# Down products in two halves of 256 columns, and sums of weight quarters on GpSimd

## The chip, the cores and the metric

The kernel runs on one core of one Trainium2 chip, in one launch. The metric is the device time of that launch in microseconds (us); lower is better. A core has TensorE (matrix products, PE in the profile; PEld is its weight loads), VectorE (DVE), ScalarE (ACT), GpSimd (POOL) and SyncE (SP), which issues the DMA transfers. Each engine works through its own queue in order, and semaphores tie the queues together.

## The reference, cut to what matters

One decoder block on 512 tokens of width 2048, all in float32: a projection, two attention mixers, an output projection, and then the feed-forward part (FFN), which the change touches:

```python
FFN_HIDDEN = 5632
...
    hn2 = rmsnorm(h, norm2_g[l])
    h = h + (jax.nn.silu(hn2 @ w_gate[l]) * (hn2 @ w_up[l])) @ w_down[l]
return rmsnorm(h, final_g)
```

## The kernel before, in words

**Three matmuls for one product.** A float32 operand is split into a high part in the format fp32r and a low part, the rest. A product of two operands is high x high, high x low and low x high, added up in PSUM. `mm3` issues these three (lines 165 to 167), and `mm` issues the same three for the gate and up products (lines 1010 to 1012). `ah` and `al` hold the high and low parts of the activations.

**Weights: jobs.** Weights come from memory as raw tiles by DMA on SyncE's queue (`load_to`, line 108, 512 KB each, four buffers `raw`; the down weights at line 736 into two buffers `rawd`). A `Job` makes one tile of 128 x 512 weights ready: `first` lets ScalarE write the high part `wh` (line 136), `second` lets VectorE write the low part `wl` = raw - high (line 139). A job may have a `prep`, issued before its high part, and a `post`, issued after its low part. `split_to` issues the jobs in a fixed order, three or four tiles ahead of TensorE; `wh` and `wl` have five buffers each. Nothing else plans the order: it is the order in which the program issues, engine by engine, and `later` puts evaluation steps some tiles behind the product they belong to. `wsplit` places the tile in its buffer at one of two offsets; jobs marked `even` take the other offset. In the FFN these are the first tile of blocks 1, 2, 5, 13, 21, 29 and 37.

**FFN by blocks.** The hidden width is cut into 44 blocks `f` of 128. For each block gate and up are one product of a 2 x 2 arrangement (two halves of the weights' rows, gate and up as columns; two halves of the tokens, 256 each), done with seven products P1 to P7 in place of eight. Each uses two weight tiles (halves `k`), so that a block has 14 tiles, each of 12 matmuls with 128 x 256 moving columns. The seven products need sums of the weight quarters A11, A21, A22, A12, which are formed in place in the raw tiles: `comb` (line 754). The order of products in a block is P1, P7, P4, P6, P5, P2, P3, and `quad_jobs` attaches the sums so: A11 += A21 ahead of P7, A21 += A22 behind P4's low part, A22 += A11 ahead of P6, A12 += A22 ahead of P3, each for both halves. In block 0 most sums are made by accumulating DMAs issued on GpSimd's queue instead (`fetch`, line 758, and line 112); one sum, ahead of P4, uses `comb` there too.

**Down products.** Four blocks' results lie in `ah[:, 12:16, :]`. In the block after them (blocks 4, 8, ..., 40) 16 down products for the 16 blocks of the model width are interleaved between the seven products; three or four follow each of P7 to P2. `down` takes one weight tile and fills one PSUM bank of 512 columns with 12 matmuls; one tile later VectorE adds the bank to `hs` (line 1077). The last four blocks' down products are made in `last`, which works in halves of 256 columns already and has 24 sums of squares on GpSimd (line 1125).

**After a product.** `after` combines the products' PSUM banks on VectorE (lines 1033, 1036, 1055: one operand in PSUM) and multiplies by the norm factor (line 1060, both operands in SBUF); `finish` makes silu (line 1017), gate x up (line 1020), and the high and low part of the result (lines 1021 and 1025).

Of the kernel before, what the change touches and what calls it, by code (L numbers as in the profile page):

```python
# [14 lines left out]
OP = mybir.AluOpType  # L15
# [8 lines left out]
PH = 4  # L24
# [47 lines left out]
def block_kernel(ctx: ExitStack, tc: tile.TileContext, xt, wst, wdn, smalls, wg, w2c, bias, ident_in, out):  # L72
# [3 lines left out]
    pe, act, dve, pool_e, sp = nc.tensor, nc.scalar, nc.vector, nc.gpsimd, nc.sync  # L76
# [13 lines left out]
    ah = slot["h"][:, MH:MH + KB * S].rearrange("p (a b) -> p a b", b=S)  # L90
    al = slot["l"][:, ML:ML + KB * S].rearrange("p (a b) -> p a b", b=S)
# [10 lines left out]
    def load_to(n):  # L102
        while state["dma"] < min(n, len(units)):
            u = state["dma"]
            t = wp.tile([128, 1024], F32, tag="raw", name="raw", bufs=LA)
            for k in range(2 if u < TWO else 1):
                c = slice(512 * k, 512 * k + 512) if u < TWO else slice(0, 1024)
                sp.dma_start(t[:, c], wst[u][:, c])
            raws[u] = t
            state["dma"] += 1  # L110
            if units[u] == ("quad", 0, 1):
                pool_e.dma_start(t, wst[u + 1], accum_op=OP.add)
# [51 lines left out]
    def mm3(o, wh, wl, mh, ml, start, stop):  # L164
        pe.matmul(o, wh, mh, start=start, stop=False)  # L165
        pe.matmul(o, wh, ml, start=False, stop=False)  # L166
        pe.matmul(o, wl, mh, start=False, stop=stop)  # L167
# [4 lines left out]
    def next_half():  # L172
        i = pos["half"]
        pos["half"] += 1
        split_to(i + (AHEAD[i] if i < len(AHEAD) else 3 if i < len(jobs) - KB - 1 else 4))
        if i < n_plain:
            load_to(i // 2 + LA)
        while lag and lag[0][0] <= i:
            lag.popleft()[1]()
        j = jobs[i]  # L180
        return j.h, j.l

    def later(n, f):
        i = len(lag)
        while i and lag[i - 1][0] > pos["half"] + n:
            i -= 1
        lag.insert(i, (pos["half"] + n, f))
# [109 lines left out]
    for k in range(KB):  # L297
        x = xc.pop(k)
# [353 lines left out]
    def proj_block(upto=None):  # L652
        return ps.tile([128, 512], F32, tag="proj", name="pp", bufs=2)
# [40 lines left out]
    for j in range(NH):  # L694
# [5 lines left out]
        p = proj_block()  # L700
# [3 lines left out]
        o = {}  # L704
# [4 lines left out]
        p = proj_block()  # L709
# [3 lines left out]
        p = proj_block()  # L713
# [5 lines left out]
        p = proj_block()  # L719
# [20 lines left out]
    def load_fin(n):  # L740
        while len(fin) < min(n, KB // 2):
            k = 2 * len(fin)
            fin.append(wp.tile([128, 1024], F32, tag="raw", name="fin", bufs=LA))
            sp.dma_start(fin[-1].rearrange("p (n c) -> p n c", n=2), wdn[NPH - 1, k:k + 2].rearrange("n p c -> p n c"))

    def quad_jobs(f, order):

        u = base_u + 4 * f

        def q(i, k):  # L750
            return raws[u + i][:, 512 * k:512 * k + 512]

        def comb(o, x):
            return lambda: dve.tensor_tensor(o(), o(), x(), op=OP.add)  # L754

        def fetch(o, i, k):

            return lambda: pool_e.dma_start(o(), wst[u + i][:, 512 * k:512 * k + 512], accum_op=OP.add)

        def nxt(i):  # L760
            return lambda: load_to(u + 4 + i + 1)

        r = {}
        for k in range(2):
            A11, A21, A22, A12 = (lambda i=i, k=k: q(i, k) for i in range(4))

            if f == 0:
                r["P1", k] = Job(A11, load=None if k else nxt(-1), post=fetch(A11, 1, k))
                r["P5", k] = Job(A21, post=fetch(A21, 0, k))
                r["P7", k] = Job(A11)  # L770
                r["P2", k] = Job(A12)
                r["P4", k] = Job(A22, prep=comb(A12, A21))
                r["P6", k] = Job(A21)
                r["P3", k] = Job(A12)
            else:
                r["P1", k] = Job(A11)
                r["P7", k] = Job(A11, prep=comb(A11, A21))
                r["P4", k] = Job(A22, post=comb(A21, A22))
                r["P5", k] = Job(A21)
                r["P6", k] = Job(A22, prep=comb(A22, A11))  # L780
                r["P2", k] = Job(A12)
                r["P3", k] = Job(A12, prep=comb(A12, A22))
        if f + 1 < FB:
            if f == 0:
                r["P6", 1].post = nxt(2)
                r["P3", 1].post = nxt(3)
            else:
                r["P6", 1].post = nxt(0)
                r["P5", 1].post = nxt(1)
                r["P3", 1].post = nxt(3)  # L790
        else:
            r["P6", 1].post = lambda: load_fin(1)
            r["P5", 1].post = lambda: load_fin(2)
            r["P3", 1].post = lambda: load_fin(LA)
        r["P1", 0].even = f in (1, 2) or f % 8 == 5
        return [r[p, k] for p in order for k in range(2)]
# [14 lines left out]
    for f in range(FB):  # L811
        qj = quad_jobs(f, ORDER if f else ORDER0)
        p = f // PH - 1
# [16 lines left out]
    def out_unit(half, tag="proj"):  # L830
        p = ps.tile([128, 512], F32, tag=tag, name="pab", bufs=2)
        c = 8 - 8 * half
        run_unit([(p, ah[:, c + k, :], al[:, c + k, :], k == 0, k == 7) for k in range(8)])
        return p
# [54 lines left out]
    for nb in range(KB):  # L889
        while "hs" not in rest and (nb == 4 and not idle() or nb == 2 and (queue or cur["s"])):  # L890
            step()
        p = out_unit(1, ("proj", "sc", "t")[nb // 2 % 3])
# [13 lines left out]
    LO, HI = slice(0, 256), slice(256, 512)  # L906
# [72 lines left out]
    for i in range(KB):  # L979
        nb = PASS2[i]  # L980
        p = out_unit(0)
# [27 lines left out]
    def mm(o, wh, wl, mh, ml, start, stop):  # L1009
        pe.matmul(o, wh, mh, start=start, stop=False, skip_group_check=True)  # L1010
        pe.matmul(o, wh, ml, start=False, stop=False, skip_group_check=True)  # L1011
        pe.matmul(o, wl, mh, start=False, stop=stop, skip_group_check=True)  # L1012
# [50 lines left out]
    def down(ph, nb):  # L1063
        n = nb % (3 if ph else 2)
        if n not in dbanks:
            dbanks[n] = banks["P3"] if not n else (ps.tile([128, 512], F32, tag="t", name="pd", bufs=2) if n == 1 else
                                                ps.tile([128, 512], F32, tag="misc", name="pd"))
        p = dbanks[n]
        h, l = next_half()
        for i in range(PH):  # L1070
            mm3(p, h[:, 128 * i:128 * i + 128], l[:, 128 * i:128 * i + 128], ah[:, 12 + i, :], al[:, 12 + i, :],
                i == 0, i == PH - 1)

        def add():
            if not ph:
                dve.tensor_tensor(hs[:, nb, :], hs[:, nb, :], st["inv"], op=OP.mult)
            dve.tensor_tensor(hs[:, nb, :], hs[:, nb, :], p, op=OP.add)  # L1077

        later(1, add)

    for kind, a, b in sched:
        if kind == "d":
            down(a, b)
            continue
        f, name = a, b
        product(f, name)
        if f == 0:
            if name == "P7":
                r = st["rs2"] = Rsqrt(tokens(sacc), D, rab.v[:, :4])
                r.invert()  # L1090
                dve.tensor_tensor(r.z, r.z, rab.y[:, :4], op=OP.mult)
                later(1, lambda r=r: st.update(inv=Spread(r.z), r2=Spread(r.y)))
            if name == "P6":
                st["inv"] = st["inv"](False)
                act.activation(st["rs2"].rs[:, 7, :1], ones[:, :1], AF.Silu)
                st["r2"] = st["r2"](tag="t", bufs=2)
                st["u"] = ft()
            if name in ("P1", "P6", "P3"):
                later(0 if name == "P1" else 1, lambda name=name: after(0, name))
        elif name in ("P1", "P6", "P5", "P2", "P3"):  # L1100
            later({(FB - 1, "P2"): 0, (FB - 1, "P3"): 3}.get((f, name), 1), lambda f=f, name=name: after(f, name))
# [144 lines left out]
```

## Time and profile before

| | |
|---|---|
| median of 3 runs | 2187.98 us (2187.74 to 2190.23) |
| the profiled execution, its time | 2189.1 us |
| its span, first to last instruction | 2187.3 us |
| mean granted TensorE clock | 0.997 |
| VectorE's sums, line 754 | 346, 237.4 us busy |
| down products in PSUM, matmuls of 512 columns in the loop | 160 x 12 |
| DMA | 33.0% of 16 engines' span, 105 GB/s |

A row of the groups gives line, engine and operation, what is written and read with its shape, the count, then busy time in us and the mean duration in ns, then the engine's idle time before it and what ended most of it. A row of the timeline gives start and duration in us, engine, line and operation. Consecutive instructions of one engine overlap at their ends: a duration is longer than the distance from start to start. For TensorE the distance between starts is called the pace here. A row of a tile's view gives shortest, median and longest duration in ns.

### The profile page before, as it was taken

Reading aid. Unit: us, or ns where it says so; the run is one execution under the profiler, and the core shown is the slowest. Engines: PE = TensorE matmul, PEld = TensorE weight load, DVE = VectorE, ACT = ScalarE, POOL = GpSimd, SP = SyncE. Lnnn points to the kernel's source line nnn. Section 1 sums busy time; section 2 is a strip of 40 time slices with the busy share of each in tenths; the row PEclk is TensorE's granted clock in tenths of the full one; section 3 lists DMA queues with packets and bytes.
Section 4 is the critical chain, followed back from the end, with each engine's and each line's share of the span. In section 5 each row is a group of like instructions: output and inputs, shape, how many; then the busy total and the mean of one; then the engine's idle time right before and its main releaser. Section 6 shows DMA issues by size and latency. Waiting matters only on the chain.

```text
span 2187.3 us, 35901 instructions
## 1 busy us (share of the span) xinstructions
PE 2167.3 (99%) x13856; PEld 1947.6 (89%) x13856; DVE 1568.5 (72%) x3045; ACT 971.0 (44%) x1862; POOL 43.7 (2%) x51
## 2 busy tenths in 40 slices
PE   9999999999999999999999999999999999999997
PEld 7788888888887889989899999989898999999897
DVE  6755656356667578979687777868696877778685
ACT  6544444344444255535343443435353434434356
POOL 0000000000000000000000000000000000000003
PEclk9999999999999999999999999999999999999998
DMA  6442222322224334333333333333333333333233
GB/s 223 145 137 80 80 80 68 101 88 80 65 92 154 98 97 106 121 111 97 107 107 111 92 116 107 102 93 122 109 97 107 107 111 97 112 106 102 90 120 106
DMA packets 82972, 232.04 MB, mean 106 GB/s; under 512 B 8816, under 2 KB 13296, under 8 KB 82800
## 3 DMA queue, kind: packets, MB, share of 16 engines
q1 hardware_dynamic: 82080, 228.17, 33.0%
q0 software_dynamic: 720, 1.57, 0.5%
q8 instruction: 109, 1.79, 0.3%
q14 instruction: 63, 0.52, 0.1%
HBM read 225.51 MB, written 4.19 MB: 105 GB/s over the span
## 4 chain that ended last, share of the span: by engine, by line
PE 96%; DVE 2%; ACT 1%; DMA 0%; issue 0%; SPq 0%; DVEq 0%; ACTq 0%
PE P L1010 13%; PE P L1011 13%; PE P L1012 13%; PE pp L165 6%; PE pp L167 6%; PE pp L166 6%; PE pd L167 4%; PE pd L166 4%; PE pd L165 4%; PE P L167 3%; PE P L166 3%; PE pab L166 3%; PE pab L167 3%; PE pab L165 3%; PE P L165 3%; PE pt L515 1%
## 5 line engine op out<-in xcount | busy, mean ns | idle before, releaser
L136 ACT ACTIVATE wh<-raw 128x512 fp32r<-128x512 f32 x888 | 549.4, 630 | 513.6 <-PE P L1011 172.0
L139 DVE TENSOR_TENSOR wl<-raw,wh 128x512 fp32r<-128x512 f32 x888 | 597.1, 686 | 62.7 <-ACT wh L136 62.2
L1012 PE MATMUL P<-ah,wl 128*128 128x256 f32 x1056 | 291.7, 276 | 0.3 <-DVE wl L139 0.3
L1010 PE MATMUL P<-ah,wh 128*128 128x256 f32 x1056 | 291.7, 276 | 0.0
L1011 PE MATMUL P<-al,wh 128*128 128x256 f32 x1056 | 291.6, 276 | 0.0
L165 PE MATMUL pp<-ah,wh 128*128 128x512 f32 x640 | 260.4, 407 | 0.0
L167 PE MATMUL pp<-ah,wl 128*128 128x512 f32 x640 | 250.9, 392 | 0.0
L166 PE MATMUL pp<-al,wh 128*128 128x512 f32 x640 | 250.2, 391 | 0.0
L754 DVE TENSOR_TENSOR raw<-raw 128x512 f32<-128x512 f32 x346 | 237.4, 686 | 3.4
L136 ACT ACTIVATE wh<-rawd 128x512 fp32r<-128x512 f32 x160 | 101.3, 633 | 280.5 <-PE pd L166 162.6
L1011 PEld LDWEIGHTS P<-al,wh 128*128 128x128 f32 x1056 | 198.2, 188 | 0.9
L1010 PEld LDWEIGHTS P<-ah,wh 128*128 128x128 f32 x1056 | 198.2, 188 | 0.8
L1012 PEld LDWEIGHTS P<-ah,wl 128*128 128x128 f32 x1056 | 198.2, 188 | 0.5 <-DVE wl L139 0.5
L1077 DVE TENSOR_TENSOR hs<-hs,pd 128x512 f32<-128x512 f32 x98 | 67.4, 688 | 131.4 <-PE pd L167 131.3
L167 PE MATMUL pd<-ah,wl 128*128 128x512 f32 x392 | 154.4, 394 | 0.0
L166 PE MATMUL pd<-al,wh 128*128 128x512 f32 x392 | 153.7, 392 | 0.0
L165 PE MATMUL pd<-ah,wh 128*128 128x512 f32 x392 | 152.1, 388 | 0.0
L167 PEld LDWEIGHTS pp<-ah,wl 128*128 128x128 f32 x640 | 120.2, 188 | 27.9
L165 PEld LDWEIGHTS pp<-ah,wh 128*128 128x128 f32 x640 | 120.5, 188 | 19.6
L166 PEld LDWEIGHTS pp<-al,wh 128*128 128x128 f32 x640 | 120.6, 188 | 19.5
L139 DVE TENSOR_TENSOR wl<-rawd,wh 128x512 fp32r<-128x512 f32 x160 | 109.8, 686 | 23.8 <-ACT wh L136 23.5
L504 ACT ACTIVATE e<-e,st 128x512 f32<-128x512 f32 (+1 forms) x96 | 54.2, 565 | 135.2 <-DVE st L502 135.2
(281 smaller groups left out, 4922.4 us busy)
## 6 DMA issues: line engine op xcount, KB each, us to landing
raw<-in_wst_dram SPq DMA_DIRECT2D x311, 512.0 KB, 3.5
rawd<-in_wdn_dram SPq DMA_DIRECT2D x160, 256.0 KB, 2.6
bias<-in_bias_dram SPq DMA_DIRECT2D x16, 320.0 KB, 3.0
xc<-in_xt_dram SPq DMA_DIRECT2D x16, 256.0 KB, 2.9
hs<-in_xt_dram SPq DMA_DIRECT2D x16, 256.0 KB, 5.2
fin<-in_wdn_dram SPq DMA_DIRECT2D x8, 512.0 KB, 3.7
out_dram<-hs SPq DMA_DIRECT2D x10, 256.0 KB, 2.2
out_dram<-hs SPq DMA_DIRECT2D x3, 512.0 KB, 3.4
```

Of the source, the lines that this page charges most:

```text
L136: act.activation(self.h, self.src(), AF.Copy)
L139: dve.tensor_tensor(self.l, self.src(), self.h.bitcast(F32), op=OP.subtract)
L165: pe.matmul(o, wh, mh, start=start, stop=False)
L166: pe.matmul(o, wh, ml, start=False, stop=False)
L167: pe.matmul(o, wl, mh, start=False, stop=stop)
L504: act.activation(et, et, AF.Exp, bias=m, scale=-1.0, accum_out=den)
L515: pe.transpose(p[:, 128 * (o + b):128 * (o + b) + 128], self.e[t][:, 128 * b:128 * b + 128], ident)
L754: return lambda: dve.tensor_tensor(o(), o(), x(), op=OP.add)
L1010: pe.matmul(o, wh, mh, start=start, stop=False, skip_group_check=True)
L1011: pe.matmul(o, wh, ml, start=False, stop=False, skip_group_check=True)
L1012: pe.matmul(o, wl, mh, start=False, stop=stop, skip_group_check=True)
L1077: dve.tensor_tensor(hs[:, nb, :], hs[:, nb, :], p, op=OP.add)
```

## The change

Two edits. In `quad_jobs`, `comb` issues its sums on GpSimd instead of VectorE; jobs and order are the same. In `down`, the bank is filled in two passes over the four weight slices, first the columns 0 to 255 (`LO`), then 256 to 511 (`HI`), by `mm` instead of `mm3` (the same three matmuls, in the form that the gate and up products use): 24 matmuls of 256 columns in place of 12 of 512.

```diff
--- before
+++ after
@@ -751,7 +751,7 @@
             return raws[u + i][:, 512 * k:512 * k + 512]
 
         def comb(o, x):
-            return lambda: dve.tensor_tensor(o(), o(), x(), op=OP.add)
+            return lambda: pool_e.tensor_tensor(o(), o(), x(), op=OP.add)
 
@@ -1067,9 +1067,10 @@
         p = dbanks[n]
         h, l = next_half()
-        for i in range(PH):
-            mm3(p, h[:, 128 * i:128 * i + 128], l[:, 128 * i:128 * i + 128], ah[:, 12 + i, :], al[:, 12 + i, :],
-                i == 0, i == PH - 1)
+        for c in (LO, HI):
+            for i in range(PH):
+                mm(p[:, c], h[:, 128 * i:128 * i + 128], l[:, 128 * i:128 * i + 128], ah[:, 12 + i, c],
+                   al[:, 12 + i, c], i == 0, i == PH - 1)
```

## The prediction

> **What bounds the kernel now.** I read the page first: the span, and how much of it TensorE is busy.
>
> ```profile
> span 2187.3 us, 35901 instructions
> ## 1 busy us (share of the span) xinstructions
> PE 2167.3 (99%) x13856; PEld 1947.6 (89%) x13856; DVE 1568.5 (72%) x3045; ACT 971.0 (44%) x1862; POOL 43.7 (2%) x51
> ```
>
> TensorE sets the time; VectorE has 28% to spare and GpSimd does nothing. The profiled execution took 2189.1 us, 1.8 us more than its span, and stands 1.1 us above the median of 2187.98; I add my sum to the median. A change of 0.2% (4.4 us) is about what can be told from none.
>
> Both edits lie in the feed-forward part, so next I read TensorE's rows in the timeline there, at the first matmul of two blocks that have no down products, two blocks apart.
>
> ```profile
> 1108.76 0.28 PE L1010 MATMUL P<-B11h,wh 128*128 128x256 f32 x1
> ...
> 1146.84 0.28 PE L1010 MATMUL P<-B11h,wh 128*128 128x256 f32 x1
> ```
>
> Two blocks take 38.08 us, one 19.04: 168 matmuls at 113.3 ns, without a pause. So VectorE's relief can save nothing in such a block; it can only be lost again.
>
> **Part 1: the halves.** 160 down products (10 phases of 16; the last phase has its own code) are 1920 matmuls of 512 columns now, and 3840 of 256 after. The pace of the wide form, 36 matmuls from the first row to the second; then that of the narrow form with the very operand of the edit, `ah[:, 12+i, c]`, in the last phase, 144 matmuls:
>
> ```profile
> 931.03 0.39 PE L165 MATMUL P<-ah,wh 128*128 128x512 f32 x1
> ...
> 939.27 0.28 PE L1010 MATMUL P<-T4h,wh 128*128 128x256 f32 x1
> ```
> ```profile
> 2130.80 0.28 PE L165 MATMUL pl<-ah 128*128 128x256 f32 x1
> ...
> 2147.11 0.28 PE L165 MATMUL pl<-ah,T1h 128*128 128x256 f32 x1
> ```
>
> 8.24/36 = 228.9 ns against 16.31/144 = 113.3 ns. Two halves take 226.6 ns, 2.3 ns less than one whole: 1920 x 2.3 = 4.4 us saved, all of it on the path. Weights are loaded twice as often, as the products do already at this pace; a weight tile is let go at its 23rd of 24 matmuls instead of its 11th of 12, 0.1 us later, which costs nothing while tiles are ready ahead. The add at L1077 waits for the whole bank as before. The Trainium skill's page "TensorE: Matmul & The Clock Gate", section "Back-to-back issue gap", gives an isolated gap of N/2.4 + 2.5 ns, by which two halves cost 2.5 ns more than one whole; the estimate from that would be +4.8 us instead of -4.4. The rows say otherwise, as long as TensorE keeps this pace.
>
> It doesn't always. Around 876 us, in the first block after block 0:
>
> ```profile
> 872.86 0.28 PE L1010 MATMUL P<-T4h,wh 128*128 128x256 f32 x1
> ...
> 875.58 0.28 PE L1010 MATMUL P<-ah,wh 128*128 128x256 f32 x1
> ...
> 876.26 0.39 PE L1012 MATMUL P<-ah,wl 128*128 128x256 f32 x1 [0.30 <-DVE wl L139]
> ...
> 878.96 0.28 PE L1010 MATMUL P<-T1h,wh 128*128 128x256 f32 x1
> ...
> 881.79 0.28 PE L1010 MATMUL P<-B21h,wh 128*128 128x256 f32 x1
> ...
> 890.23 0.28 PE L1010 MATMUL P<-ah,wh 128*128 128x256 f32 x1
> ...
> 892.95 0.28 PE L1010 MATMUL P<-T4h,wh 128*128 128x256 f32 x1
> ```
>
> Up to 875.58 24 matmuls take 2.72 us (113.3 ns). Then P6 waits for a low part on VectorE. From 878.96 on 24 take 2.83 us (117.9 ns), and from 890.23, after the first tile of block 2, which is placed `even`, 2.72 again. So a pause on TensorE puts the narrow form into a slower pace, 4.6 ns a matmul, until the next `even` tile, which comes with blocks 1, 2, 5, 13, 21, 29 and 37 only. No other pause happens in this part before.
>
> **Part 2: the sums on GpSimd.** What leaves VectorE, and what a block without downs has there (the window is one block; the 15th L139 is a neighbour's):
>
> ```profile
> L754 DVE TENSOR_TENSOR raw<-raw 128x512 f32<-128x512 f32 x346 | 237.4, 686 | 3.4
> ```
> ```profile
> L139 DVE TENSOR_TENSOR wl<-raw,wh 128x512 fp32r<-128x512 f32 x15 | 10.1, 687 | 1.0 <-ACT wh L136 1.0
> L754 DVE TENSOR_TENSOR raw<-raw 128x512 f32<-128x512 f32 x8 | 5.5, 687 | 0.1
> L1033 DVE TENSOR_TENSOR ft<-ft,P 128x256 f32<-128x256 f32 x3 | 1.3, 419 | 0.1
> L1036 DVE TENSOR_TENSOR ft<-ft,P 128x256 f32<-128x256 f32 x2 | 0.8, 421 | 0.1
> L1020 DVE TENSOR_TENSOR ft<-ft 128x512 f32<-128x512 f32 x1 | 0.7, 684 | 0.0
> L1025 DVE SCALAR_TENSOR_TENSOR al<-ft,ah 128x512 fp32r<-128x512 f32 x1 | 0.7, 684 | 0.0
> L1060 DVE TENSOR_TENSOR ft<-ft,r 128x256 f32<-128x256 f32 x1 | 0.4, 424 | 0.0
> L1055 DVE TENSOR_TENSOR ft<-P,r 128x256 f32<-128x256 f32 x1 | 0.4, 414 | 0.0
> ```
>
> 346 = 43 x 8 + 2: two sums of block 0 (before its P4) move too. On GpSimd the same form, seen before only in attention, and what VectorE does beside it:
>
> ```profile
> L649 POOL TENSOR_TENSOR acc<-acc,osq x14: 1276/1316/1930, 250.5 to 678.7; 128x512 f32<-128x512 f32 x14
> ```
> ```profile
> 263.65 1.28 POOL L649 TENSOR_TENSOR acc<-acc,osq 128x512 f32<-128x512 f32 x1 [11.74 <-ACT osq L648]
> ...
> 264.12 1.36 DVE L438 TENSOR_TENSOR qbl<-tmp,qbh 128x512 fp32r<-128x512 f32 x1 [2.79 <-ACT qbh L437]
> ```
>
> One sum takes 1.28 us when undisturbed, against 0.69. And VectorE's instruction, which reads two SBUF tensors like L139 (0.69 us), took 1.36: it ended at 265.48, 0.55 us after GpSimd's end at 264.93. It stood still while GpSimd ran. This is the rule against this change: the Trainium skill's "SBUF — State Buffer", section "SBUF: two separate sides", says that VectorE and GpSimd share a port pair as an exclusive lock, held for a whole instruction by a VectorE operation with two SBUF inputs or by GpSimd's. The trace agrees: 1.36 us instead of 0.69; had the two engines shared the port without loss, the sum would be Part 1 alone.
>
> So the two engines take turns. Budget of a block without downs: GpSimd 8 x 1.28 = 10.2 us; VectorE's two-SBUF instructions (14 L139, L1020, L1025 at 0.55 behind a turn of GpSimd, L1060 0.4) 9.2 us. Sum 19.4, against 19.04 for TensorE. The six PSUM instructions (L1033, L1036, L1055; under 0.42 each, 2.5 in all) can lie beside GpSimd where the order allows.  Blocks with downs (one in four, 44 us longer on TensorE) have ample room. So each three blocks in a row start with full lead and use it up.
>
> How much lead is there? Block at 1127.81:
>
> ```profile
> 1127.94 0.64 ACT L136 ACTIVATE wh<-raw 128x512 fp32r<-128x512 f32 x1 [0.72 <-PE P L1011]
> ...
> 1128.89 0.69 DVE L139 TENSOR_TENSOR wl<-raw,wh 128x512 fp32r<-128x512 f32 x1
> ...
> 1133.24 0.28 PE L1010 MATMUL P<-T4h,wh 128*128 128x256 f32 x1
> ...
> 1134.44 1.89 DVE L139 TENSOR_TENSOR wl<-raw,wh 128x512 fp32r<-128x512 f32 x3
> ...
> 1135.96 0.28 PE L1010 MATMUL P<-ah,wh 128*128 128x256 f32 x1
> ```
>
> P4's first high part starts when TensorE frees its buffer, 5.3 us before its matmuls. The tight place is P6, the one that paused at 876: between P4's first low part and P6's second stand four of the eight sums, alternating with low parts. P6's second tile starts at 1135.96 + 1.36 = 1137.32 and needs its low part at the third matmul, 1137.55; today that (the first of the three at 1134.44) is done at 1135.1, 2.4 us early. In turns, from the start of P1: the first P4 sum ends at 0.8, P7's second low part at 1.4, L1033 and L1060 at 2.1, P4's low parts at 2.7 and 3.3, P6's first sum at 4.4, L1020 at 5.0, P4's second sum at 6.1, P6's first low part at 6.7, P6's second sum at 7.8, its high part (0.64) at 8.5, its low part at 9.1. Needed at 9.7: 0.7 us left in the first block after the downs. Carried on the same way the turns need, as an estimate, 19.85 us a block (19.4 and the gaps in which one engine waits for the other's result), 0.8 more than TensorE: -0.1 in the second block, -0.9 in the third. TensorE pauses about once per three blocks, at P6, and the pause brings the 117.9 ns. At that pace a block takes 19.8 us, and the turns about keep up: the loss is mostly the pace.
>
> GpSimd's queue: its DMA issues of block 0 (five, the last at 846) stand ahead of the sums, the 24 adds of the last phase (L1125) behind them; nothing else waits there. A later sum also frees weights later, and SyncE waits for that:
>
> ```profile
> SPq L108 <- DVE raw L754: 497.9, 83, 14.6
> ```
> ```profile
> raw<-in_wst_dram SPq DMA_DIRECT2D x311, 512.0 KB, 3.5
> ```
> ```profile
> 1120.64 0.68 DVE L754 TENSOR_TENSOR raw<-raw 128x512 f32<-128x512 f32 x1
> ```
>
> The last sum of a block ends at 1121.3 and P4 of the next reads the new weights at 1127.94: 6.6 us for a load of 3.5. A sum up to 3 us later is hidden; I find 0.3 to 2.4. Cost nothing; if the cover is gone it is the same pause at P4.
>
> Sum. Slow pace: first from P6 of block 3 to block 4, then in each stretch between `even` tiles from P6 of the second block (6 and so on) on: 6.6 of 8 blocks x 168 x 4.6 ns = 5.1 us, and two phases of downs, 384 x 117.9 ns = 45.3 instead of 192 x 228.9 ns = 43.9 each, 2.7: 7.8 us, four times, 31; the short stretches at both ends 2.5 + 5.6; the last phase up to its norm 192 x 4.6 ns = 0.9. Together 40. The six pauses that begin it at 0.46 us (876.26 - 875.69, less 0.11) 3, later ones 2. +45: 2188 + 45 = 2233. Bounds of this case: pauses in only half of the stretches, the others with Part 1's gain, 2188 + 22 - 2 = 2208; turns of 20.4 us a block, 33 x 0.6 us more than the slow pace covers, 2253.
>
> **Rivals.** *No pause* (0.16): the order lets GpSimd run ahead, the 0.7 us hold; for it: 28% spare on VectorE, the P6 slack of 2.4; against: 19.4 us of turns in 19.04. Then only Part 1 is left, 2183.6, on either side of the 0.2%; this one ends on the other side. It decides at P6's second low part of the third block: earlier than TensorE by any margin. *Halves that cost* (0.03, also without pauses): a fixed cost per matmul comes back in the down order; at 117.9 ns in the downs alone, 3840 x 117.9 - 1920 x 228.9 = +13 us, 2201. The page's gap gives 2193 there. *Pauses, but the pace holds* (0.13): up to 0.1 + 0.9 us per three blocks, 11 times, to twice that, less 4.4: 2195 to 2206. For it: only one pause in this part is on record. *Heavy turns* (0.15): the PSUM instructions don't overlap and a block takes 19.4 + 2.5 = 21.9 us: 33 blocks x 2.9 less 11 x 1 us of lead, 85, and the slow pace in ten blocks with downs, 10 x (0.8 + 1.4) = 22: 2188 + 107 = 2295; half overlapped some 2255. *Turned pace*, the forecast: 0.53.
>
> **The numbers.** 2233, the likeliest. No pause is left out below (0.16), and the far end of heavy turns above (0.04): 2190 to 2275. No pause splits evenly at 0.2%: faster 0.08, same 0.08, slower 0.84.
>
> **What would show it.** Right: POOL busy near 500 us with L754 above 1.28 us; L139's mean above 687 ns; TensorE waits for `wl` at P6 in the second or third block of a cycle; 117.9 ns behind them until the next `even` tile; down halves at 113.3 ns only where no pause came before. Wrong: blocks of 19.04 us throughout and 2183; or L139 still at 687 ns beside GpSimd, so that the lock is not held against this form; or pauses after which 113.3 ns goes on.

## The result, and the profile after

The changed kernel takes 2289.88 us (median of 4 runs, 2288.57 to 2290.33) against 2188.06 before: ratio 1.0462, 95% interval 1.0449 to 1.0474, slower by 102 us. That is above the range; the direction was right. The profiled execution took 2290.33 us, its span 2288.6, so 101.3 us lie between the two profiled spans. The sums below are for the feed-forward part, where 99.9 of them arise.

The head of the page, then the groups of VectorE and GpSimd over the whole span:

```profile
span 2288.6 us, 39977 instructions
## 1 busy us (share of the span) xinstructions
PE 2227.3 (97%) x15776; PEld 2078.9 (91%) x15776; DVE 1532.1 (67%) x2699; ACT 955.4 (42%) x1862; POOL 554.6 (24%) x397
```
```profile
L139 DVE TENSOR_TENSOR wl<-raw,wh 128x512 fp32r<-128x512 f32 x888 | 722.9, 835 | 155.2 <-ACT wh L136 146.6
L754 POOL TENSOR_TENSOR raw<-raw 128x512 f32<-128x512 f32 x346 | 511.0, 1495 | 864.8 <-DVE wl L139 552.9
```

The 346 sums went over to GpSimd as said (511.0 us busy there), and VectorE lost instructions but hardly any busy time (1532.1 after 1568.5): its L139 went from 687 ns to 835. From here on only the feed-forward part is compared, from block 1's first matmul to the first `pl` matmul of the last phase. VectorE's groups there, after:

```profile
L139 DVE TENSOR_TENSOR wl<-raw,wh 128x512 fp32r<-128x512 f32 x600 | 530.6, 905 | 138.7 <-ACT wh L136 130.6
...
L1020 DVE TENSOR_TENSOR ft<-ft 128x512 f32<-128x512 f32 (+1 forms) x44 | 66.0, 1499 | 0.0
L1033 DVE TENSOR_TENSOR ft<-ft,P 128x256 f32<-128x256 f32 x131 | 54.4, 416 | 4.4 <-PE P L1012 1.8
```

Two SBUF operands: 905 and 1499 ns, from 687 and 679. One operand in PSUM (L1033): 416, from 419, untouched.

What TensorE waited for, in all, how often, and the longest:

```profile
PE P L1010 <- ACT ah L1021: 22.2, 10, 2.7
PE P L1012 <- DVE wl L139: 14.6, 17, 1.5
...
PE P L1011 <- DVE al L1025: 4.2, 10, 0.4
```

The second row is P6, where the forecast had its pauses. The first and third are new: at the first down product of each of the ten phases TensorE waits for `ah` and `al`, the moving operand.

To account for all of it I took each distance between two neighbouring matmul starts, less 113.33 ns for a narrow and 228.9 ns for a wide one. A small excess (up to 30 ns) is pace; distances of 200 to 225 ns are counted as narrow matmuls at half the clock; all else is a pause. (Some 15 of the 144 in the column of the halved clock, 1.6 us, lie where the granted clock is full, and are short waits.)

| feed-forward part, us | length | pace | halved clock | pauses |
|---|---|---|---|---|
| before | 1259.8 | 0.9 | 0.1 | 0.6 |
| after | 1359.7 | 39.3 | 14.5 (144 matmuls) | 52.1 |

With the 4.3 us that the halves save at full pace, 39.3 + 14.5 + 52.1 - 4.3 - 1.6 = 100.0; measured 99.9. Of the pauses 17.4 are P6's (17 times) and 30.8 the first downs' (23.8 for `ah`, 7.0 for `al`).

**P6.** The timeline of block 2, TensorE's rows, then VectorE's, then GpSimd's:

```profile
893.12 0.28 PE L1010 MATMUL P<-T4h,wh 128*128 128x256 f32 x1
...
895.84 0.28 PE L1010 MATMUL P<-ah,wh 128*128 128x256 f32 x1
...
897.29 0.39 PE L1012 MATMUL P<-ah,wl 128*128 128x256 f32 x1 [1.06 <-DVE wl L139]
...
899.99 0.28 PE L1010 MATMUL P<-T1h,wh 128*128 128x256 f32 x1
...
902.81 0.28 PE L1010 MATMUL P<-B21h,wh 128*128 128x256 f32 x1
```
```profile
892.46 1.38 DVE L139 TENSOR_TENSOR wl<-raw,wh 128x512 fp32r<-128x512 f32 x1 [0.62 <-ACT wh L136]
893.76 1.78 DVE L1020 TENSOR_TENSOR ft<-ft 128x512 f32<-128x512 f32 x1
895.46 1.77 DVE L139 TENSOR_TENSOR wl<-raw,wh 128x512 fp32r<-128x512 f32 x1
```
```profile
891.99 4.70 POOL L754 TENSOR_TENSOR raw<-raw 128x512 f32<-128x512 f32 x3 [2.09 <-DVE wl L139]
```

Three sums on GpSimd stretch three VectorE instructions of 0.69 us to 1.38, 1.78 and 1.77. GpSimd ends at 896.69 and the last L139 at 897.23, 0.54 us later: turns. TensorE reads that low part at 897.29 instead of 896.07, and 24 matmuls take 2.82 us from 899.99 where they took 2.72 from 893.12: behind the pause the slow pace has begun.

The same kind of pause can also end the slow pace. In block 15:

```profile
1304.06 0.28 PE L1010 MATMUL P<-T4h,wh 128*128 128x256 f32 x1
...
1306.89 0.28 PE L1010 MATMUL P<-ah,wh 128*128 128x256 f32 x1
...
1308.09 0.39 PE L1012 MATMUL P<-ah,wl 128*128 128x256 f32 x1 [0.81 <-DVE wl L139]
...
1310.69 0.28 PE L1010 MATMUL P<-T1h,wh 128*128 128x256 f32 x1
...
1313.41 0.28 PE L1010 MATMUL P<-B21h,wh 128*128 128x256 f32 x1
```

Here 24 matmuls take 2.83 us before the pause and 2.72 after it, and no tile of this block is `even`. This happens at five of the 17 pauses (at 1308, 1697, 1827, 2086 and 2216 us).

**The first down product of a phase,** block 8; TensorE, ScalarE and VectorE of after, then the same instructions of before (there the first of L165 in the down is the row at 1051.22):

```profile
1064.73 0.28 PE L1010 MATMUL P<-ah,wh 128*128 128x256 f32 x1
...
1067.90 0.39 PE L1010 MATMUL P<-ah,wh 128*128 128x256 f32 x1 [1.95 <-ACT ah L1021]
1068.71 0.39 PE L1011 MATMUL P<-al,wh 128*128 128x256 f32 x1 [0.42 <-DVE al L1025]
...
1069.24 0.42 PE L1011 MATMUL P<-al,wh 128*128 128x256 f32 x1
...
1072.23 0.40 PE L1010 MATMUL pd<-ah,wh 128*128 128x256 f32 x1
```
```profile
1062.29 1.07 DVE L1060 TENSOR_TENSOR ft<-ft,r 128x256 f32<-128x256 f32 x1
```
```profile
1066.70 0.63 ACT L136 ACTIVATE wh<-rawd 128x512 fp32r<-128x512 f32 x1 [2.15 <-DMA rawd<-in_wdn_dram]
1067.23 0.61 ACT L1021 ACTIVATE ah<-ft 128x512 fp32r<-128x512 f32 x1
```
```profile
1051.22 0.39 PE L165 MATMUL P<-ah,wh 128*128 128x512 f32 x1
...
1053.28 0.39 PE L165 MATMUL P<-ah,wh 128*128 128x512 f32 x1
```
```profile
1046.43 0.43 DVE L1060 TENSOR_TENSOR ft<-ft,r 128x256 f32<-128x256 f32 x1
```
```profile
1051.31 0.61 ACT L1021 ACTIVATE ah<-ft 128x512 fp32r<-128x512 f32 x1
```

The fourth slice of `ah` comes from the block just before, through L1060, silu, L1020 and L1021. Before, it was done at 1051.92 and read at 1053.28, behind nine wide matmuls: 1.36 us to spare. After, three things happen. The read comes behind nine narrow matmuls, since the first half goes through all four slices before the second half starts: 1.06 us after the product's start instead of 2.06, so 1.00 us is gone. The turns put L1060 2.44 us ahead of the product's start instead of 4.79: 2.35 gone. From L1060 to the end of L1021 it is 5.55 us, 0.06 more; L1021 stands in ScalarE's queue behind a high part that waits for a down tile's load, as it did before. 1.36 - 1.00 - 2.35 - 0.06 = -2.05, and TensorE waits 2.1 us. Then L1025, the low part, makes it wait 0.7 us more. Behind the two pauses 14 matmuls take 2.99 us, 213.6 ns each; the windows view gives the granted clock (the column before the last two):

```profile
1068.90:1072.40 3.50, 3.50 (x18) 3.50 (x18) 1.64 (x3) 0.89 (x2) 2.84 (x2) 0.52 0.28 80
```

The granted clock was 0.52 in these 3.5 us. The Trainium skill's page "TensorE: Matmul & The Clock Gate", section "Part 1: The HAM clock gate (the "warmup" mystery)", says that idle time halves the array's clock, to exactly N divided by 1.2 GHz from start to start, as an estimate 213.3 ns here; the trace agrees with 213.6. It gives the idle window as some 3.4 us; here pauses of 2.1 and 0.7 us, one matmul apart, were enough; the last section says how they add up.

### The profile page after: what moved, and what is told of

Its sections match the earlier page's. It is cut to its first block, busy times and chain, and to the rows that moved or that the text cites. A ratio compares the mean times of both kernels' runs of the same rounds, so it can differ in the third digit from the quotient of the medians.

```text
span 2288.6 us, 39977 instructions
## 1 busy us (share of the span) xinstructions
PE 2227.3 (97%) x15776; PEld 2078.9 (91%) x15776; DVE 1532.1 (67%) x2699; ACT 955.4 (42%) x1862; POOL 554.6 (24%) x397
## 4 chain that ended last, share of the span: by engine, by line
PE 78%; DVE 9%; issue 5%; DMA 3%; POOL 2%; ACT 2%; DVEq 0%; SPq 0%; ACTq 0%; POOLq 0%
PE P L1011 10%; PE P L1012 10%; PE P L1010 10%; PE pp L165 6%; PE pp L167 6%; PE pp L166 6%; DVE wl L139 5%; PE pd L1010 4%; PE pd L1012 4%; PE pd L1011 4%; PE pab L166 2%; PE pab L167 2%; PE pab L165 2%; POOL raw L754 2%; ACT wh L136 2%
## 5 line engine op out<-in xcount | busy, mean ns | idle before, releaser
L139 DVE TENSOR_TENSOR wl<-raw,wh 128x512 fp32r<-128x512 f32 x888 | 722.9, 835 | 155.2 <-ACT wh L136 146.6
L754 POOL TENSOR_TENSOR raw<-raw 128x512 f32<-128x512 f32 x346 | 511.0, 1495 | 864.8 <-DVE wl L139 552.9
L1010 PE MATMUL P<-ah,wh 128*128 128x256 f32 x1552 | 439.1, 283 | 22.2 <-ACT ah L1021 22.2
L1012 PE MATMUL P<-ah,wl 128*128 128x256 f32 x1552 | 441.1, 284 | 14.6 <-DVE wl L139 14.6
L1011 PE MATMUL P<-al,wh 128*128 128x256 f32 x1552 | 440.5, 284 | 4.2 <-DVE al L1025 4.2
L165 PE MATMUL pp<-ah,wh 128*128 128x512 f32 x640 | 260.4, 407 | 0.0
L1010 PE MATMUL pd<-ah,wh 128*128 128x256 f32 x784 | 219.8, 280 | 0.0
L1011 PE MATMUL pd<-al,wh 128*128 128x256 f32 x784 | 219.4, 280 | 0.0
L1012 PE MATMUL pd<-ah,wl 128*128 128x256 f32 x784 | 219.3, 280 | 0.0
L1010 PEld LDWEIGHTS pd<-ah,wh 128*128 128x128 f32 x784 | 148.2, 189 | 0.0
L1011 PEld LDWEIGHTS pd<-al,wh 128*128 128x128 f32 x784 | 147.8, 188 | 0.0
L1012 PEld LDWEIGHTS pd<-ah,wl 128*128 128x128 f32 x784 | 147.5, 188 | 0.0
```

The lines of the kernel that those rows point to most:

```text
L139: dve.tensor_tensor(self.l, self.src(), self.h.bitcast(F32), op=OP.subtract)
L754: return lambda: pool_e.tensor_tensor(o(), o(), x(), op=OP.add)
```

## The experiments

Terms in the table below are counted as above. All times are medians of runs next to runs of the kernel before.

### Each edit alone

Only the halves (`down` of the change, sums on VectorE):

> Only the down products' halves; the sums stay on VectorE. Theory A (the operand is wanted too early): with the halves outermost, the fourth slice, which is the result of the block just ended, is read after 9 narrow matmuls (1.0 us) instead of 9 wide ones (2.1 us). In the trace of before L1025 ends 1.4 us after the first down product begins, so TensorE pauses some 0.3 us at each of the ten first down products, and each pause brings the slow pace (117.9 ns) until the next even tile: +3 for the pauses, some +37 for the pace, -4.4 for the halves: about 2224 us. Theory B (the halves are only cheaper): no pause, 113.3 ns throughout, 2183.6 us.

Measured 2201.53 us, ratio 1.0073 (1.0031 to 1.0114), between the two theories, and the runs lie far apart, 2191.67 to 2221.51. In the profiled one TensorE paused at one of ten first downs:

```profile
1051.32 0.36 PE L1010 MATMUL P<-ah,wh 128*128 128x256 f32 x1
1052.10 0.39 PE L1011 MATMUL P<-al,wh 128*128 128x256 f32 x1 [0.42 <-DVE al L1025]
```

The distance is 0.78 us, 0.67 too long; the slow pace that follows lasts to 1486 and costs 17.2 us, all pauses together 1.4. So the order of columns alone uses the slack up to the edge, without GpSimd.

Only the sums on GpSimd (`comb` of the change, `down` as before):

> Only the sums on GpSimd; the down products stay 512 wide. Theory A (turns on the port, and the late operand): pauses at P6 as after the change (17 us), slow pace in the products (some 24 us), the wide down products 226.7 ns in that state (-4), the first down products pause only some 1.7 us each instead of 3 (17 us in all), and the granted clock drops less after them (0 to 14 us): 2242 to 2256 us. Theory B (the sums explain all, the halves only save 4.4): 2289.9 + 4.4 = 2294 us.

2252.93 us, ratio 1.0294 (1.0279 to 1.0309): theory A. Its waits:

```profile
PE P L1012 <- DVE wl L139: 14.0, 16, 1.5
PE P L165 <- ACT ah L1021: 9.4, 10, 1.1
PE P L166 <- DVE al L1025: 3.1, 10, 0.3
```

The first downs wait here too, but 1.1 us and not 2.1, and the clock stays up (granted 1.00 from 867 to 2180 us). Some 65 of the 101.8 us are the sums' own. The halves, which alone cost 13, cost 37 on top of them.

### The order of the halves

Halves alone, with the slices outermost. With a `start` in each half, the second one drops the first slice's share of columns 0 to 255, which this kernel and the next therefore leave out:

```diff
-        for c in (LO, HI):
-            for i in range(PH):
+        for i in range(PH):
+            for c in (LO, HI):
```

> Only the halves, but with the slices outermost: for each slice first the columns 0 to 255, then 256 to 511; the sums on VectorE. The fourth slice is then read after 18 narrow matmuls (2.0 us), as late as before. Theory A: no pause, 2183.6 us, 40 us faster than the halves outermost. Theory B: 2183.6 us too, but the same as the halves outermost. If narrow matmuls in the down products bring the slow pace by themselves: about 2201 us and more, with either order.

2184.10 us, ratio 0.9978 (0.9968 to 0.9988). This is the median of ten executions; one of them took 4627 us, and no trace shows why (without it the median is 2183.95). Both theories gave this time; that narrow matmuls in the down products cost by themselves, 2201 us and more, is ruled out. The same edit in the changed kernel:

> The changed kernel with the slices outermost in the down products, so that the fourth slice is read 1.0 us later. Theory A: each of the ten pauses at the first down product shrinks by about 1 us, and the drop of the granted clock behind it is shorter or gone: 14 to 28 us faster than the changed kernel, 2262 to 2276 us. Theory B (the pauses have nothing to do with when the operand is read): 2290 us.

2262.68 us, ratio 1.0339 (1.0324 to 1.0355): theory A. So the order of columns is 27.2 us of the changed kernel's 101.8. Of `ah`'s 23.8 us of pauses 10.5 are left, and the granted clock no longer dips (1.00 from 867 to 2190 us); the slow pace (40.6) stays.

Halves alone, slices outermost and one `start` in the bank, so that the whole sum is made:

```diff
-                   al[:, 12 + i, c], i == 0, i == PH - 1)
+                   al[:, 12 + i, c], i == 0 and c == LO, i == PH - 1)
```

> The halves with the slices outermost and the sums on VectorE, as before, but only the first matmul of a bank starts an accumulation; the first one of the columns 256 to 511 doesn't. If a start clears the whole bank's record of what was written, as the missing share of the first slice in the columns 0 to 255 suggests, this computes the reference, and its time is that of the run with two starts, 2184 us: 1920 x 2.3 ns = 4.4 us less than before. If the narrow form has a cost of its own that the last run missed: 2188 us or more.

2183.59 us (11 runs), ratio 0.9982 (0.9974 to 0.9991), 4.6 us faster than before: Part 1's 4.4. This version beats both kernels.

### The load ahead of L1021

A third buffer for the down weights' raw tiles, loaded early, in the changed kernel (`bufs=2` to `bufs=3` at line 735 and one more `load_dn()`):

> The changed kernel with three buffers for raw down weights in place of two. Theory A (the pause at the first down product: ScalarE's L1021 stands in its queue behind the high part of the third down tile, which waits for a load that could start only when the first down tile's low part was done): the load comes earlier, the ten pauses fall from 3.1 us to some 1.2, and the halved clock behind them goes: 45 us become 12, 2257 us. Theory B (the pause is the turns alone, L1060 and L1020 late): 2290 us.

2261.49 us, ratio 1.034 (1.0325 to 1.0356), close to theory A. Its waits:

```profile
PE P L1013 <- DVE wl L139: 16.9, 18, 1.5
PE P L1011 <- ACT ah L1022: 7.6, 10, 1.3
```

```profile
1063.01 0.63 ACT L1022 ACTIVATE ah<-ft 128x512 fp32r<-128x512 f32 x1 [0.84 <-DVE ft L1021]
```

The slice of block 8 (L1022 here) now waits for its data alone, not behind a load. The wait for `ah` falls as far as with the order mended (9.3 us in my count), and of the ten dips of the clock one is left. Either mend is worth 27 to 28 us: what both take away is about 1 us of each wait, and with it nearly all the dips of the clock.

### Where the slow pace ends

The changed kernel with an `even` tile in each block at P5 (`r["P5", 0].even = f > 0`):

> The changed kernel, with the first tile of P5 (the one behind the pause at P6) placed even in every block but the first. Theory A (an even tile ends the slow pace): the 39 us of slow pace shrink to some 10, those between the first down product and P5 of the same block; the turns on the port take part of it back as longer pauses at P6: 2262 to 2280 us. Theory B (the placement doesn't set the pace, or a pause undoes it at once): 2290 us.

2281.6 us, ratio 1.0423 (1.0409 to 1.0437). It fell short: the pace term went from 39.3 to 20.8, but pauses rose from 52.1 to 62.1 and the halved clock to 15.7. A TensorE that runs faster comes to the same late tiles earlier; that this is why the pauses grew is argued, not shown. Both mends, this edit and one start together:

> All sums on GpSimd, with every mend found: slices outermost with one start, three buffers for raw down weights, P5's first tile even. Theory A (pauses at the first down product, slow pace and pauses at P6 are separate terms): the first down product pauses some 0.3 us, the slow pace costs some 20 us, P6 some 25 us, the halves give 4.4 back: about 2233 us, still slower than before, for the turns stay. Theory B (each mend only moves the wait to the next place): 2260 us as with one mend.

2244.16 us, ratio 1.0254 (1.0238 to 1.027), between the theories: pace 23.8, pauses 33.7, of which P6 23.2.

### Turns, by themselves

The kernel before, with an added GpSimd sum into a scratch tile (`pool_e.tensor_tensor(scr["t"], scr["t"], o(), op=OP.add)`) behind each sum on VectorE; nothing reads its result:

> The kernel before, with all its sums on VectorE, and behind each sum of blocks 1 to 43 one GpSimd add of the same form into a scratch tile that nothing reads. Theory A (turns on a shared port): nobody waits for GpSimd's result, but VectorE stands still 8 x 1.3 us a block; turns of 10.2 + 9.2 + 8 x 0.55 = 23.8 us a block against 19.04: 33 blocks x 4.8 us less the lead, and the slow pace: 2330 to 2380 us, L139 and L754 well above 0.7 us. Theory B (the cost of the change is only that a sum takes 1.3 us instead of 0.7 in the chain): 2188 us, L139 at 687 ns.

2399.43 us, ratio 1.0965 (1.0948 to 1.0982): theory A, and 19 us above its range. The same with a GpSimd memset of the tile, which reads nothing, and a VectorE instruction of 0.15 us on one column to space them:

> As the run with scratch adds, but GpSimd only writes the scratch tile (a memset, which reads nothing); a tiny VectorE instruction that reads one column of the tile behind each sum spaces the memsets as the adds were spaced. Theory A1 (VectorE's two-input instructions and GpSimd's exclude each other only where GpSimd reads): L139 and the sums stay at 0.69 us; 2188 us, a little more for the 344 tiny instructions. Theory A2 (any GpSimd instruction takes the shared port): L139 rises above 0.69 us by a good part of the memset's length, and the time by tens of us.

2188.71 us, ratio 1.0000 (0.9990 to 1.0009): theory A1. The groups of the adds' kernel, then of the memsets', both in the feed-forward part:

```profile
L757 POOL TENSOR_TENSOR scr<-scr,raw 128x512 f32<-128x512 f32 x344 | 556.6, 1618 | 929.3 <-issue 671.1 <-DVE raw L755 255.6
L139 DVE TENSOR_TENSOR wl<-raw,wh 128x512 fp32r<-128x512 f32 x600 | 511.0, 864 | 28.7 <-ACT wh L136 28.5
```
```profile
L139 DVE TENSOR_TENSOR wl<-raw,wh 128x512 fp32r<-128x512 f32 x600 | 405.8, 685 | 31.6 <-ACT wh L136 21.2
...
L758 POOL MEMSET scr<- 128x512 f32 x343 | 180.7, 527 | 1074.6 <-DVE scro L757 1074.6
```

No product reads a result of either, yet L139 goes to 864 ns with the adds and stays at 685 with the memsets. The memsets do meet it: 264 of the L139 overlap one by more than 0.1 us, and the longest of these takes 694 ns. So GpSimd at work is not what stops VectorE; an add that reads SBUF does, a memset that only writes it doesn't. The Trainium skill's "SBUF — State Buffer", section "SBUF: two separate sides", says just this, that a VectorE operation with two SBUF inputs takes the lock only against a GpSimd operation that reads SBUF; the trace agrees.

### Fewer sums on GpSimd, and how little starts the slow pace

From the 2183.59 us version, four of a block's eight sums on GpSimd (ahead of P7 and P3), and then two (behind P4):

```diff
+        def comb(o, x, e=dve):
+            return lambda: e.tensor_tensor(o(), o(), x(), op=OP.add)
...
+                r["P7", k] = Job(A11, prep=comb(A11, A21, pool_e))
...
+                r["P3", k] = Job(A12, prep=comb(A12, A22, pool_e))
```

> The halves with slices outermost and one start; of the eight sums of a block only the four ahead of P7 and P3 on GpSimd, the four between P4 and P6 on VectorE. Turns: 4 x 1.28 + 9.2 + 4 x 0.6 = 16.7 us a block, below TensorE's 19.04. Theory A (the sum of the turns in a stretch decides): no pause at P6; 2184 us, or up to 2200 where L1025 comes too late for the first down product (its margin of 0.9 us is less than one turn). Theory B (any sum on GpSimd costs its share): half of the 65 us that all sums cost: 2216 us.

> The same, with only the two sums behind P4 on GpSimd (A21 += A22, wanted only by P5, four tiles later). Turns 2 x 1.28 + 9.2 + 6 x 0.6 = 15.4 us a block. Theory A: no pause; these two lie in the tight stretch up to P6, which has 2.4 us to spare, and take some 1.4 us more there: 2184 us, the same as without them. Theory B: a quarter of 65 us: 2200 us.

2226.2 us, ratio 1.0172 (1.0154 to 1.019), and 2227.61, ratio 1.0172 (1.0156 to 1.0188). Both theories missed both (2184 and up to 2200 against 2216 for the first, 2184 against 2200 for the second): half the sums cost 42.6 us and a quarter 44.0. In the account, pauses are 1.2 and 3.3 us, the pace 39.4 and 39.9. The four-sums kernel at the first down of block 16, TensorE's rows and VectorE's:

```profile
1303.71 0.28 PE L1010 MATMUL P<-ah,wh 128*128 128x256 f32 x1
1303.92 0.39 PE L1011 MATMUL P<-al,wh 128*128 128x256 f32 x1
...
1304.62 0.28 PE L1010 MATMUL pd<-ah,wh 128*128 128x256 f32 x1
...
1307.44 0.28 PE L1010 MATMUL pd<-ah,wh 128*128 128x256 f32 x1
```
```profile
1303.18 0.68 DVE L1025 SCALAR_TENSOR_TENSOR al<-ft,ah 128x512 fp32r<-128x512 f32 x1
```

L1025 ends at 1303.86, and the matmul that reads it starts 0.21 us after its neighbour, 0.10 late. Then 24 matmuls take 2.82 us, up to the `even` tile of block 29, at 1737 us. Is that wait the whole cost, or do sums on GpSimd slow the pace by themselves? The next kernel is the same, but the down products begin one product later, behind P4. They then end behind P3, and the last ones of a phase read the next group's first slice in place of their own: that share of the computation is changed in the three kernels of this kind.

```diff
-            if f and f % PH == 0 and i:
-                for _ in range(3 if i < 5 else 4):
+            if f and f % PH == 0 and i > 1:
+                for _ in range(3 if i < 6 else 4):
```

> Halves with the slices outermost and one start; only the sums ahead of P7 and P3 on GpSimd; and the down products begin one product later, behind P4 instead of behind P7. Theory A: in the kernel with the same four sums and the downs behind P7, the waits at the first down product add up to about 1 us, and the 40 us of its cost is the slow pace (117.8 ns) that each of them starts; one product later the fourth slice is ready some 2.7 us earlier than it is read, no wait comes, and the pace stays at 113.3 ns: 2184 to 2190. Theory B: the sums themselves slow TensorE down (a shared path to SBUF), wherever the downs lie: 2226.

2185.92 us, ratio 0.998 (0.9971 to 0.999): theory A. In block 16 its downs go at full pace, 2.72 us for 24, though L139 still meets GpSimd's sums (770 ns):

```profile
1299.14 0.28 PE L1010 MATMUL pd<-ah,wh 128*128 128x256 f32 x1
...
1301.86 0.28 PE L1010 MATMUL pd<-ah,wh 128*128 128x256 f32 x1
```
```profile
L139 DVE TENSOR_TENSOR wl<-raw,wh 128x512 fp32r<-128x512 f32 x600 | 453.1, 770 | 115.5 <-ACT wh L136 105.9
```

Its control, with all sums on VectorE:

> Halves with the slices outermost and one start, sums on VectorE, down products one product later. The control for the two others: 2184 by both theories, as with the downs behind P7; if the later place costs something by itself, this shows how much.

2184.39 us, ratio 0.998 (0.9971 to 0.999). So four sums on GpSimd cost nothing that can be told where no wait comes of them, and bring nothing. And the changed kernel with its downs one product later:

> The changed kernel with one edit: the down products begin one product later, behind P4 instead of behind P7 (columns still outermost, all sums on GpSimd). Theory A: the waits for the fourth slice at the ten first downs (31 us) and the halved clock behind them (14.5 us) are a matter of that place alone; they go, and the waits at P6 and the slow pace stay: 2240 to 2250. Theory B: the waits there are time that the turns of the two engines have to cost somewhere; they come back at the next tile that is late: 2270 to 2290.

2253.42 us, ratio 1.0284 (1.0268 to 1.03), 3 us above theory A. Its one large wait in this part:

```profile
PE P L1012 <- DVE wl L139: 19.1, 29, 1.5
```

The first downs' waits are gone, and so are the dips of the clock (granted 1.00 in this part). A little comes back at P6, 29 pauses in place of 17 (23.9 us for 17.4): presumably the pause at the first down had given the turns time.

| | time, us | pace | halved clock | pauses (P6; first downs) |
|---|---|---|---|---|
| changed kernel | 2289.88 | 39.3 | 14.5 | 52.1 (17.4; 30.8) |
| slices outermost | 2262.68 | 40.6 | 1.8 | 35.5 (15.7; 17.5) |
| third buffer | 2261.49 | 36.8 | 3.7 | 37.0 (19.8; 15.4) |
| downs later | 2253.42 | 39.0 | 2.2 | 27.0 (23.9; 0) |
| sums alone | 2252.93 | 27.5 | 1.9 | 35.4 (16.6; 16.8) |
| two sums, behind P4 | 2227.61 | 39.9 | 0.4 | 3.3 |
| four sums, downs later | 2185.92 | 2.5 | 0.1 | 0.7 |

Entries of 2.2 us and less under halved clock are short waits, for the granted clock does not dip in this part of those runs; in the third buffer's 3.7 us is one dip.

## Why the prediction was wrong

**The slow pace: right in kind, and in size partly by luck.** The forecast put 40 us on it with the down halves' saving already in; in the same terms it is 39.3 - 4.3 and about 1 in the last phase, 36. It starts at pauses, as forecast. But it ends as often at a pause (five times) as at an `even` tile (blocks 2, 5, 21, 29 and 37), the `even` tile of block 13 leaves it slow, and a pause of 0.8 us at 1027 left it fast. The forecast had pauses only start it and every `even` tile end it.

**The turns: right in kind.** VectorE's L139 ends 0.54 us behind GpSimd, PSUM instructions are untouched (66 of the L1033 overlap one of GpSimd's sums by more than 0.1 us and take 419 ns on average, 423 at most), and POOL is busy 554.6 us with L754 at 1495 ns. No pause for a load was added at P4. The rival of heavy turns gave 2295 us, near the measured time, but by another cause: it let L1033, L1036 and L1055 wait for GpSimd, and L1033 takes 416 ns.

**P6's pauses: the step failed that said "At that pace a block takes 19.8 us, and the turns about keep up".** They were to cost 5 us, and cost 17.4. They come in the second and third block behind the downs, as the budget had it, and the budget's own 0.9 us for the third block was near the 0.97 us measured there most often. But the sum took six of them at 0.46 us, the size of the one seen before, and 2 us for the rest. There are 17 of about a microsecond each, and the slow pace doesn't absorb them: GpSimd's sums were reckoned at 1.28 us each and take 1.495 in turns, and L1020 1.5 us.

**The halves' timing: the step failed that looked at the weight tile ("costs nothing") and the bank ("as before") and left out the third operand.** The order of columns brings the read of the fourth slice of `ah` forward by 1.0 us, where 1.36 were to spare for the high part and 0.8 for the low. This, with L1060 2.35 us later by the turns, makes the waits at ten first downs: 30.8 us, and the 14.5 of halved clock. The forecast had neither place nor clock; it gave the blocks with downs "ample room", and all ten of these waits lie in them. Of the 57 us missed, 45 are these two and 12 P6; the other pauses are 4, and the pace term 4 less than forecast.

What isn't settled: why a pause puts the narrow form into the slower pace or takes it out, why an offset of the weight tile takes it out, and why each sometimes does nothing.

## What to carry to other kernels

When a loop's order changes, work out when each operand is first read: weights, accumulator and moving operand, and against the latest producer of its last slice. Where a kernel has a pace that any wait can end, price the first wait and not the sum of waits, and look for every place with under a microsecond of slack. Work taken from VectorE to GpSimd frees VectorE only as far as its instructions with two SBUF operands don't meet GpSimd's that read SBUF.

## What the runs showed of the hardware that was not expected

- A wait of 0.10 us on TensorE is enough to start the slow pace (24 matmuls in 2.82 us after 2.72); waits in four phases, the longest 0.4 us, came before the four-sums kernel's 40 us of slow pace, and without the waits (downs later) it is gone. In the feed-forward part of the changed kernel pauses start the slow pace ten times and end it five times.
- Pauses halve the granted clock if enough of them fall together. The ten dips of the changed kernel last 3.41 us each, and they begin at whole multiples of 3.413 us from one another (129.71 us is 38 of them). I divided the feed-forward parts of eight traces (the changed kernel, sums alone, slices outermost, third buffer, `even` tiles, all mends, downs later, scratch adds) into stretches of that length in step with the dips, and added up the pauses (those of over 0.05 us) in each stretch at full clock: behind all 33 with 2.13 us or more comes a dip, and of the others behind one alone, with 2.06 us. So single pauses of 1.7 us at P6 bring none, 1.05 and 0.7 us (slices outermost) none, and in the `even` kernel 2.50 and 0.69 us at 1196 us, which fall into two stretches, none either (granted clock 1.00).
- A GpSimd memset of 128 x 512 (527 ns) leaves VectorE's two-operand instructions at 685 ns; a GpSimd add of the same size takes 1618 ns beside them, and they 864.
